# Graph aggregation by one-hot products: two PSUM banks for the moved products, tables and selectors on other engines, and a new order of the first lists

## The chip, the cores and the metric

One NeuronCore of a Trainium2 chip runs the kernel. The metric is device time in microseconds, the median of three runs. The profile is that of one execution, taken by the hardware profiler.

## The reference

Each of 65536 edges adds the feature row of its source node to the output row of its destination node. There are 4096 nodes with 128 float32 features each.

```python
num_nodes, num_edges, dim = 4096, 65536, 128
output = np.zeros((num_nodes, dim), dtype=np.float32)
for i in range(len(edge_index_src)):
    output[edge_index_dst[i]] += node_features[edge_index_src[i]]
```

## The kernel before

The kernel has no gather and no scatter. It sorts the edges with products of one-hot matrices, and then forms the output as a product of dense count blocks with the features. A node number is split into a block of 128 nodes (`>> 7`, 32 blocks) and a place in it (`& 127`).

**Preparation, first pass.** The edges lie on 128 partitions in six lists (`q` = 0 to 5, `NQ = 6`), each a column group of up to 22 × 4 edges per partition. The indices arrive by three transfers each for source and destination: list 0, list 1, and lists 2 to 5 together. For each list the kernel does the following, with the engine in brackets:

- `dst_keys(q)` [VectorE] shifts the destination to its block number. `buckets1(q)` [VectorE] compares it with a table of 32 block numbers and writes the one-hots `oh1`. The tables (`psi`, four slots of one PSUM bank) come from index vectors that GpSimd makes; `more_iotas` [VectorE] copies three of them there.
- `column_sums1(q)` [TensorE, L253] adds up the one-hots into `pst`, and `scan(q)` [VectorE, L265] runs a prefix sum over them.
- `count(q, n)` steps a generator: matmuls of the one-hots with a triangle [TensorE, L273 and L275; L307 and L311 for list 0] into `psc`, evicted by ScalarE (L278, L314) into `cum`. Lists 1 to 5 have eleven evictions, in six steps. The rest of the generator sums the four edges of a column group with the `lists` selector [TensorE, L292; L319 for list 0, 32 matmuls] and `take_ranks` [ScalarE, L299] copies the ranks out, twice.
- `codes()` [VectorE, L202, L204 and L206] packs the 7-bit places of source and destination and the source block number; `words(a, b)` [ScalarE, L212] turns these into the 32-bit words `kab` of lists a to b; `spread1(q)` [GpSimd, L333] multiplies the one-hots with them, in four instructions.
- `move1(q)` permutes the words to their rank: four groups `l`, each with three one-hots `p` of the rank [VectorE, L236] and about 22 products [TensorE, L356] into the PSUM tile `psm`, and at the end two copies [ScalarE, L360 and L361] out of `psm` into `sbk` and `sa`.

The order on each engine is written out by hand, and each engine works off its instructions in that order. While `move1(q)` goes on, `during(q)` puts work of later lists between its four groups: at `l = 0` the column sums of list q + 3, at `l = 1` the end of `count(q + 1)` (so its ranks) and `scan(q + 3)`, and two steps of `count(q + 2)` in each of the last three groups. `beside(q, l)` adds the start of the second pass, among it `sums0(2)` [TensorE, L461] in the last group of list 3 and `scan0(2)` [VectorE, L466] in the first of list 4.

PSUM has eight banks. Here they are shared by tag: "psA" (four buffers, count matmuls, fillers and later the blocks), "ps2", "pso", "misc" (one each) and "psi" (the tables). `psm` takes "misc" except for list 4, which takes a "psA". Column sums take "ps2" for even lists and "pso" for odd ones. `T0["x"]` of the second pass takes "ps2" early in list 2. `keep_busy(n)` issues n products of ones that nobody reads.

**Preparation, second pass,** and **the block of products.** The moved edges are sorted once more by destination group (`pass2`). Then 32 slots follow: one-hots of source and destination places [VectorE, `onehots`], their products, which are count blocks [TensorE, L769], a copy by ScalarE (L771), and the products of these with the features [TensorE, L776].

Of the kernel before, what the change touches and what calls it, by code (L numbers as in the profile page):

```python
# [8 lines left out]
P = 128  # L9
# [8 lines left out]
NB = 32  # L18
# [64 lines left out]
def _fast(ctx, tc, X, src32, dst32, out, ident, fmax, flag_i, T):  # L83
# [86 lines left out]
    V.tensor_copy(out=psi[:, 0], in_=iota[:].bitcast(I32))  # L170

    def selectors():
        with nc.allow_low_precision(reason="zeros and ones"):
            for t, by in ((lists, "p (k b) -> p k b"), (dests, "p (b k) -> p k b")):
                V.tensor_reduce(out=t[:], in_=identb[:].rearrange(by, k=4), op=OP.add, axis=AX.X)

    def more_iotas(which):
        for i, t in which:
            V.tensor_copy(out=psi[:, i, :t.shape[1] // 2], in_=t.bitcast(I32))

    piota, piotas = psi[:, 0].bitcast(U16), psi[:, 1].bitcast(U16)
    pswap = psi[:, 3].bitcast(U16)
# [15 lines left out]
            in_=by_quad(d_lo)[:, q, :, :, None].to_broadcast([P, NJ, 4, 2]),  # L198
            scalar=7, op=OP.logical_shift_right)

    def codes():
        V.tensor_scalar(out=code_i, in0=s_lo, scalar1=127, scalar2=7,  # L202
                        op0=OP.bitwise_and, op1=OP.logical_shift_left)
        V.scalar_tensor_tensor(out=code_i, in0=d_lo, scalar=127, in1=code_i,  # L204
                               op0=OP.bitwise_and, op1=OP.bitwise_or)
        V.tensor_single_scalar(out=sblk_i, in_=s_lo, scalar=7, op=OP.logical_shift_right)  # L206

    def words(a, b):
# [39 lines left out]
        onehot(oh1q(q), kd[:, q], NL, NB, io=pswap if q % 2 else piota)  # L248

    def column_sums1(q):  # L250
        pst = ps.tile([P, 512], F32, name="pst", tag=("ps2", "pso")[q % 2], bufs=1)
        for j in range(NJ):
            PE.matmul(out=pst[:, j:j + 1],  # L253
                      lhsT=oh1q(q)[:, 4 * j:4 * j + 4, :].rearrange("p l b -> p (l b)"),
                      rhs=ones[:, :1], start=True, stop=True)
        sums[q] = pst
# [23 lines left out]

    def counts_by_two(q):

        cum = sb1.tile([P, NJ, P], BF16, name="cum", tag=f"c{q % 2}")
        col = oh1q(q).rearrange("p (j l) b -> p j (l b)", l=4)
        for j0 in range(0, NJ, 4):
            js = range(j0, min(j0 + 4, NJ))
            before_by_two(col[:, j0:js.stop], cum[:, j0:js.stop],
                          [sums[q][:, j - 1:j] if j else minus[:] for j in js[::2]])
            yield
        psr = ps.tile([P, 512], F32, name="psr", tag="psA", bufs=4)  # L290
        for j in range(NJ):
            PE.matmul(out=psr[:, 4 * j:4 * j + 4], lhsT=cum[:, j], rhs=lists[:],  # L292
                      start=True, stop=True)
        take_ranks(q, psr)
# [5 lines left out]

    def counts(q):

        cum = sb1.tile([P, NB, NL], BF16, name="cum", tag=f"c{q % 2}")
        for j0 in range(0, NJ, 4):
            n = min(4, NJ - j0)
            psc = ps.tile([P, 512], F32, name="psc", tag="psA", bufs=4)
# [36 lines left out]
    sbk = sb1.tile([P, NCH, NB], BF16, name="sbk")  # L343

    def move1(q, meanwhile):
        tag, bufs = ("psA", 4) if q == NQ - 2 else ("misc", 1)
        psm = ps.tile([P, 512], F32, name="psm", tag=tag, bufs=bufs)
        for l in range(4):
            t = p1[l // 2]
            n = QN[q]  # L350
            for j0, j1, m0, m1 in WIN:
                j1 = min(j1, n)
                onehot(t[:, l % 2, j0:j1, m0:m1], rank1[q][:, l, j0:j1], j1 - j0, m1 - m0, m0=m0)
            meanwhile(l)
            for j in range(n):
                PE.matmul(out=psm[:, l * 64:(l + 1) * 64], lhsT=t[:, l % 2, j, :],  # L356
                          rhs=v1[q][:, 4 * j + l].bitcast(BF16),
                          start=j == 0, stop=j == n - 1)
        pv = psm[:, :256].rearrange("p (l b k) -> p l b k", l=4, k=2)
        S.copy(out=sbk[:, place(q), :], in_=pv[:, :, :, 0])  # L360
        S.copy(out=sa[:, place(q), :], in_=pv[:, :, :, 1])  # L361
# [21 lines left out]
    def leave(k, pso):  # L383
# [6 lines left out]
        for h, copy, queue, tag in parts:  # L390
            psx = ps.tile([P, 512], F32, name="psx", tag=tag, bufs=1)
            for i in range(2):
# [4 lines left out]
                out=out[(4 * k + 2 * h) * P:(4 * k + 2 * h + 2) * P, :].rearrange(  # L397
                    "(i p) f -> p i f", p=P), in_=rows[:, 2 * h:2 * h + 2])

    dst_keys(0)  # L400
    buckets1(0)
    load_x()
    column_sums1(0)
    keep_busy(6)
    more_iotas([(1, iotas[:]), (2, iota4[:].rearrange("p s k -> p (s k)"))])
    scan(0)
    selectors()
    more_iotas([(3, iotax[:].rearrange("p s k -> p (s k)"))])
    for q in range(1, NQ):
        dst_keys(q)  # L410
    codes()
    buckets1(1)
    count(0, 4)
    words(0, 1)
    spread1(0)
    count(0, 2)
    words(1, NQ)
    keep_busy(16)
    column_sums1(1)
    spread1(1)  # L420
    buckets1(2)
    count(0)
    scan(1)
    column_sums1(2)
    buckets1(3)
    count(1, 6)
    scan(2)
    column_sums1(3)

# [5 lines left out]
    def start0():  # L435
        T0["o"] = sb1.tile([P, NCH, NB, 4], BF16, name="oh0", tag="oh0")
        both = sb1.tile([P, 2, NCH, NB, 4], BF16, name="vc0", tag="o0")
        T0["v"], T0["c"] = both[:, 0], both[:, 1]
        T0["s"] = sb1.tile([P, NCH], F32, name="sums0")
        T0["r"] = rank2[:, 0]  # L440
        T0["p"] = ps.tile([P, 512], F32, name="pst0", tag="pso", bufs=1)
        T0["x"] = ps.tile([P, 512], F32, name="ps0", tag="ps2", bufs=1)

    def keys0(q):
        cs = place(q)
# [85 lines left out]
    def beside(q, l):  # L531
# [23 lines left out]
        if (q, l) == (5, 1):  # L555
            x_part(2, 0)
        if (q, l) == (5, 2):
            ranks0(EARLY0[0], T0["x"][:, 384:], 2)
            x_part(0, 1, (0,))
            payloads0(4)  # L560
# [438 lines left out]
```

## Time and profile before

| what | value |
|---|---|
| median of three runs | 272.2 us (270.98, 272.2, 272.39) |
| the profiled execution | 271.35 us |
| its span | 269.7 us |
| TensorE, matmuls | 259.0 us busy (96%) |
| VectorE | 243.7 us busy (90%) |
| ScalarE | 192.8 us busy (71%) |
| GpSimd | 194.2 us busy (72%) |

Busy time is summed over the span from the first instruction to the last; the profiled execution's own time is 1.65 us longer than its span. The names in the profile: PE is TensorE's matmuls and PEld its weight loads, DVE is VectorE, ACT is ScalarE, POOL is GpSimd and SP is SyncE. L253 is line 253 of the kernel.

### The profile page before, as it was taken

How to read it: one execution, taken by the hardware profiler on the slowest of the kernel's cores; microseconds unless marked ns; L12 is line 12 of the kernel's file. 1: busy time of each engine (PE TensorE's matmuls, PEld its weight loads, DVE VectorE, ACT ScalarE, POOL GpSimd, SP SyncE). 2: the span in 40 equal slices, each digit the busy share in tenths (PEclk: the TensorE clock that was granted, in tenths of full speed). 3: DMA queues.
4: the chain of work that ended last, by engine and by line, in shares of the span. 5: the costliest groups of instructions: out<-in, count | busy, mean ns of one | idle time of the engine just before them, and what ended most of it. 6: DMA issues, size and time to landing. Idle time of an engine off the chain costs nothing.

```text
span 269.7 us, 7795 instructions
## 1 busy us (share of the span) xinstructions
PE 259.0 (96%) x3322; PEld 219.1 (81%) x3323; DVE 243.7 (90%) x261; ACT 192.8 (71%) x437; POOL 194.2 (72%) x198
## 2 busy tenths in 40 slices
PE   8899899889999999999999999999999999999993
PEld 7788888767888888888788888887888888878882
DVE  7999989999999999999999998999898899889601
ACT  2787799567867568785777677767777785868761
POOL 3498889999899999999899989999799200000000
PEclk9999999999999999999999999999999999999999
DMA  5900000000000010010001000100010001001001
GB/s 161 296 14 7 2 2 2 4 2 4 0 4 2 0 41 0 2 39 2 2 0 41 1 2 2 41 2 0 2 39 2 0 8 33 5 0 41 0 4 39
DMA packets 10068, 5.75 MB, mean 21 GB/s; under 512 B 304, under 2 KB 10032, under 8 KB 10032
## 3 DMA queue, kind: packets, MB, share of 16 engines
q1 hardware_dynamic: 8944, 4.59, 6.1%
q10 hardware_dynamic: 1088, 0.66, 0.9%
q8 instruction: 26, 0.43, 0.6%
q14 instruction: 10, 0.08, 0.1%
HBM read 3.15 MB, written 2.10 MB: 19 GB/s over the span
## 4 chain that ended last, share of the span: by engine, by line
PE 78%; DVE 8%; ACT 2%; issue 1%; DVEq 0%
PE pso L776 45%; PE psa L769 21%; DVE p L236 4%; PE ps L694 4%; PE psr L678 2%; PE psb L643 2%; DVE p2a L236 1%; PE psx L375 1%; DVE oh L236 1%; PE psm L356 1%; DVE oh L617 1%; DVE oh L446 0%; ACT xr L221 0%; PE psc L722 0%; PE psc L273 0%
## 5 line engine op out<-in xcount | busy, mean ns | idle before, releaser
L771 ACT CAST a<-psa 128x512 fp32r<-128x512 f32 x256 | 131.8, 604 | 26.2 <-PE psa L769 25.9
L776 PE MATMUL pso<-a,xr 128*128 128x512 f32 x512 | 134.7, 404 | 0.1
L776 PEld LDWEIGHTS pso<-a,xr 128*128 128x128 f32 x512 | 91.0, 189 | 17.0 <-ACT a L771 0.8
L236 DVE TENSOR_TENSOR oh<-psi,slo 128x4096 bf16<-128x4096 uint16 (+2 forms) x38 | 73.9, 1945 | 7.9 <-PE psa L769 7.9
L236 DVE TENSOR_TENSOR oh<-psi,dlo 128x4096 bf16<-128x4096 uint16 (+2 forms) x38 | 73.8, 1942 | 0.0
L769 PE MATMUL psa<-oh 128*128 128x128 bf16 x1024 | 68.2, 219 | 1.1 <-DVE oh L236 1.1
L769 PEld LDWEIGHTS <-oh 128*128 128x128 bf16 x1024 | 57.8, 98 | 13.1 <-issue 10.5
L626 POOL TENSOR_TENSOR v<-oh,sa 128x512 bf16<-128x512 bf16 x42 | 42.6, 1054 | 0.0
L665 POOL TENSOR_TENSOR cum<-cum,oh 128x512 bf16<-128x512 bf16 x36 | 40.6, 1169 | 0.0
L333 POOL TENSOR_TENSOR v<-oh,kab 128x704 f32<-128x704 bf16 x24 | 32.9, 1404 | 10.3 <-ACT kab L212 6.9
L236 DVE TENSOR_TENSOR p<-psi,rank 128x448 bf16<-128x448 uint16 (+3 forms) x72 | 29.6, 476 | 0.2 <-ACT rank L299 0.2
L356 PE MATMUL psm<-v,p 128*128 128x64 bf16 x512 | 19.8, 193 | 2.2 <-DVE p L236 1.8
L656 POOL TENSOR_TENSOR cum<-cum,two 128x256 bf16<-128x256 bf16 x25 | 19.3, 773 | 2.6 <-ACT cum L645 1.1
L356 PEld LDWEIGHTS <-p 128*128 128x128 bf16 x512 | 17.2, 98 | 3.7 <-DVE p L236 3.0
L278 ACT ACTIVATE cum<-psc,sums 128x256 bf16<-128x256 f32 x50 | 18.7, 504 | 0.0
L633 POOL TENSOR_TENSOR two<-oh 128x512 bf16<-128x512 bf16 x15 | 17.1, 1171 | 2.0 <-DVE oh L617 2.0
L660 POOL TENSOR_TENSOR cum<-cum,oh 128x512 bf16<-128x512 bf16 x15 | 17.0, 1161 | 0.0
L236 DVE TENSOR_TENSOR p2a<-psi,rank 128x3072 bf16<-128x3072 uint16 (+2 forms) x14 | 14.3, 1062 | 0.5 <-ACT rank L682 0.5
L236 DVE TENSOR_TENSOR p2c<-psi,rank 128x3072 bf16<-128x3072 uint16 x8 | 13.6, 1745 | 0.0
L273 PE MATMUL psc<-early,oh 128*128 128x256 bf16 x67 | 13.2, 272 | 0.2 <-ACT cum L278 0.2
L617 DVE TENSOR_TENSOR oh<-psi,sbk 128x3072 bf16<-128x3072 uint16 (+3 forms) x9 | 12.4, 1390 | 0.0
L275 PE MATMUL psc<-early,oh 128*128 128x128 bf16 x67 | 12.1, 219 | 0.0
(114 smaller groups left out, 240.8 us busy)
## 6 DMA issues: line engine op xcount, KB each, us to landing
xf<-in_node_features_dram SPq DMA_DIRECT2D x4, 512.0 KB, 5.8
out_dram<-rows SPq DMA_DIRECT2D x7, 256.0 KB, 2.2
raw<-in_edge_index_src_dram ACTq DMA_DIRECT2D x1, 336.0 KB, 5.6
raw<-in_edge_index_dst_dram SPq DMA_DIRECT2D x1, 336.0 KB, 5.4
raw<-in_edge_index_src_dram ACTq DMA_DIRECT2D x2, 88.0 KB, 2.7
raw<-in_edge_index_dst_dram SPq DMA_DIRECT2D x2, 88.0 KB, 2.5
out_dram<-rows SPq DMA_DIRECT2D x1, 128.0 KB, 1.8
out_dram<-rows ACTq DMA_DIRECT2D x1, 128.0 KB, 1.8
```

The source lines that it names most:

```text
L236: V.tensor_tensor(out=dst.rearrange("p i (m k) -> p i m k", k=2), in0=io.rearrange("p i (m k) -> p i m k", k=2), in1=keys2[:, :, None, :]. ...
L278: S.activation(out=cum[:, 2 * i:2 * i + 2].rearrange("p j e -> p (j e)"), in_=psc[:, 2 * i * P:2 * (i + 1) * P], func=RELU, bias=bias)
L333: G.tensor_tensor(out=v1[q][:, l::4], in0=oh1q(q)[:, l::4], op=OP.mult, in1=kab[:, q, l::4, None].to_broadcast([P, NJ, NB]))
L356: PE.matmul(out=psm[:, l * 64:(l + 1) * 64], lhsT=t[:, l % 2, j, :], rhs=v1[q][:, 4 * j + l].bitcast(BF16), start=j == 0, stop=j == n - 1)
L626: G.tensor_tensor(out=T2["v"][:, c:c + 4], in0=T2["o"][:, c:c + 4], op=OP.mult, in1=sa[:, c:c + 4, None, d0:d0 + 4].to_broadcast([P, 4, NB ...
L633: G.tensor_tensor(out=T2["t"][:, i:i + 4], in0=oh[:, i:i + 4, 0], in1=oh[:, i:i + 4, 1], op=OP.add)
L656: G.tensor_tensor(out=cum[:, :, 2 * i], in0=cum[:, :, 2 * i - 2], in1=two[:, :, i - 1], op=OP.add)
L660: G.tensor_tensor(out=cum[:, i:i + 4, 1], in0=cum[:, i:i + 4, 0], in1=oh[:, i:i + 4, 0], op=OP.add)
L665: G.tensor_tensor(out=flat("c")[:, c:c + 4], in0=flat("c")[:, c:c + 4], in1=flat("o")[:, c:c + 4], op=OP.mult)
L769: PE.matmul(out=psa[:, i * P:(i + 1) * P], lhsT=oh[:, 0, 4 * k + i, :], rhs=oh[:, 1, 4 * k + i, :], start=True, stop=True)
L771: S.copy(out=a[:, k, :], in_=psa[:])
L776: PE.matmul(out=pso[:], lhsT=xr[s // 16][:, s % 16, v, :], rhs=a[:, k, :], start=s == 0 and v == 0, stop=s == NB - 1 and v == 1)
```

## The change

The diff has four parts.

1. `psm` of lists 1 and 3 takes the tag "ps2"; lists 0, 2 and 5 stay in "misc" and list 4 in "psA". To make room, the column sums of list 4 go to "pso", and `T0["x"]` is allocated in list 5 instead of list 2.
2. `more_iotas` copies on ScalarE instead of VectorE. `selectors` no longer reduces on VectorE: `lists` comes from two selects, and `dests` from five additions of halves, all on GpSimd.
3. `codes` takes a range of lists: lists 0 and 1 come before the first scan, lists 2 to 5 after the second one-hots. The shift to source blocks is a function of its own, `src_blocks`, after them. `words` comes in three parts (list 0, list 1, lists 2 to 5) instead of two.
4. The order of the first lists is new: keys and one-hots of list 1 stand ahead of the keys of lists 2 to 5; column sums and scan of list 1 come sooner; the first step of its count stands ahead of the end of list 0's; its `cum` takes the tag "oh0" instead of "c1", which the raw indices hold. The fillers ahead of the counts go from 6 to 3, and those after them from 16 to 6.

```diff
     def selectors():
-        with nc.allow_low_precision(reason="zeros and ones"):
-            for t, by in ((lists, "p (k b) -> p k b"), (dests, "p (b k) -> p k b")):
-                V.tensor_reduce(out=t[:], in_=identb[:].rearrange(by, k=4), op=OP.add, axis=AX.X)
+        G.affine_select(out=lists[:], in_=ones[:, :4], pattern=[[-32, 4]], base=1,
+                        channel_multiplier=1, compare_op=OP.is_gt, fill=0.0)
+        G.affine_select(out=lists[:], in_=lists[:], pattern=[[32, 4]], base=32,
+                        channel_multiplier=-1, compare_op=OP.is_gt, fill=0.0)
+        t, n = identb, P // 2
+        while n >= 4:
+            to = dests if n == 4 else sb1.tile([P, n], BF16, name=f"fold{n}")
+            G.tensor_tensor(out=to[:], in0=t[:, :n], in1=t[:, n:], op=OP.add)
+            t, n = to, n // 2
 
     def more_iotas(which):
         for i, t in which:
-            V.tensor_copy(out=psi[:, i, :t.shape[1] // 2], in_=t.bitcast(I32))
+            S.copy(out=psi[:, i, :t.shape[1] // 2], in_=t.bitcast(I32))
...
-    def codes():
-        V.tensor_scalar(out=code_i, in0=s_lo, scalar1=127, scalar2=7,
+    def codes(a, b):
+        ts = slice(a * NL, b * NL)
+        V.tensor_scalar(out=code_i[:, ts], in0=s_lo[:, ts], scalar1=127, scalar2=7,
                         op0=OP.bitwise_and, op1=OP.logical_shift_left)
-        V.scalar_tensor_tensor(out=code_i, in0=d_lo, scalar=127, in1=code_i,
+        V.scalar_tensor_tensor(out=code_i[:, ts], in0=d_lo[:, ts], scalar=127, in1=code_i[:, ts],
                                op0=OP.bitwise_and, op1=OP.bitwise_or)
+
+    def src_blocks():
         V.tensor_single_scalar(out=sblk_i, in_=s_lo, scalar=7, op=OP.logical_shift_right)
...
-        pst = ps.tile([P, 512], F32, name="pst", tag=("ps2", "pso")[q % 2], bufs=1)
+        pst = ps.tile([P, 512], F32, name="pst", tag="ps2" if q in (0, 2) else "pso", bufs=1)
...
-        cum = sb1.tile([P, NJ, P], BF16, name="cum", tag=f"c{q % 2}")
+        cum = sb1.tile([P, NJ, P], BF16, name="cum", tag="oh0" if q == 1 else f"c{q % 2}")
...
-        tag, bufs = ("psA", 4) if q == NQ - 2 else ("misc", 1)
+        tag, bufs = {1: ("ps2", 1), 3: ("ps2", 1), NQ - 2: ("psA", 4)}.get(q, ("misc", 1))
...
+    selectors()
     dst_keys(0)
     buckets1(0)
     load_x()
     column_sums1(0)
-    keep_busy(6)
-    more_iotas([(1, iotas[:]), (2, iota4[:].rearrange("p s k -> p (s k)"))])
+    keep_busy(3)
+    more_iotas([(3, iotax[:].rearrange("p s k -> p (s k)")), (1, iotas[:]),
+                (2, iota4[:].rearrange("p s k -> p (s k)"))])
+    codes(0, 2)
     scan(0)
-    selectors()
-    more_iotas([(3, iotax[:].rearrange("p s k -> p (s k)"))])
-    for q in range(1, NQ):
+    dst_keys(1)
+    buckets1(1)
+    for q in range(2, NQ):
         dst_keys(q)
-    codes()
-    buckets1(1)
+    codes(2, NQ)
+    src_blocks()
     count(0, 4)
     words(0, 1)
     spread1(0)
+    column_sums1(1)
+    scan(1)
     count(0, 2)
-    words(1, NQ)
-    keep_busy(16)
-    column_sums1(1)
+    words(1, 2)
     spread1(1)
     buckets1(2)
+    count(1, 1)
+    keep_busy(6)
     count(0)
-    scan(1)
     column_sums1(2)
     buckets1(3)
-    count(1, 6)
+    count(1, 5)
+    words(2, NQ)
     scan(2)
     column_sums1(3)
...
-        T0["x"] = ps.tile([P, 512], F32, name="ps0", tag="ps2", bufs=1)
...
         if (q, l) == (5, 2):
+            T0["x"] = ps.tile([P, 512], F32, name="ps0", tag="ps2", bufs=1)
             ranks0(EARLY0[0], T0["x"][:, 384:], 2)
```

## Rows read from the trace of the kernel before

**Rows 1.** The chain of waits in order of time: start us, us, what.

```profile
58.71 0.62 PE psa L769 x8
```

**Rows 2.** Busy time by stretch; columns as the first line says.

```profile
core 0: us, PE busy (x) PEld busy (x) DVE busy (x) ACT busy (x) POOL busy (x), PEclk, DMA share, GB/s
...
14.10:29.00 14.90, 13.57 (x346) 12.66 (x343) 14.90 (x34) 13.12 (x40) 13.12 (x11) 1.00 0.02 6
...
68.00:265.00 197.00, 196.78 (x2053) 164.67 (x2050) 177.78 (x110) 142.76 (x303) 137.46 (x138) 1.00 0.04 11
```

**Rows 3.** Timeline of VectorE, the head: start us, us, engine, line, operation [idle before].

```profile
3.66 1.62 DVE L236 TENSOR_TENSOR oh<-psi,kd 128x2816 bf16<-128x2816 uint16 x1
...
6.15 0.20 DVE L265 TENSOR_TENSOR_SCAN sums<-ones,pst 128x22 bf16<-128x22 bf16 x1 [0.20 <-PE pst L253]
6.27 0.26 DVE L175 TENSOR_REDUCE lists<-identb 128x4 bf16<-128x128 bf16 x1
...
6.71 0.25 DVE L196 TENSOR_SCALAR kd<-raw 128x176 uint16<-128x176 uint16 x1
7.25 0.73 DVE L196 TENSOR_SCALAR kd<-raw 128x176 uint16<-128x176 uint16 x4 [0.29 <-DMA raw<-in_edge_index_dst_dram]
7.90 0.43 DVE L202 TENSOR_SCALAR raw<-raw 128x528 uint16<-128x528 uint16 x1
8.36 0.71 DVE L204 SCALAR_TENSOR_TENSOR raw<-raw 128x528 uint16<-128x528 uint16 x1
8.98 0.43 DVE L206 TENSOR_SCALAR raw<-raw 128x528 uint16<-128x528 uint16 x1
9.33 3.15 DVE L236 TENSOR_TENSOR oh<-psi,kd 128x2816 bf16<-128x2816 uint16 x2
...
14.12 0.37 DVE L236 TENSOR_TENSOR p<-psi,rank 128x448 bf16<-128x448 uint16 x1
```

**Rows 4.** Timeline of ScalarE, the head.

```profile
7.42 2.42 ACT L314 ACTIVATE cum<-psc,minus 128x512 bf16<-128x512 f32 x4 [3.58 <-PE psc L311]
9.72 0.48 ACT L212 ACTIVATE kab<-raw 128x88 uint16<-128x88 uint16 x2
10.05 1.06 ACT L314 ACTIVATE cum<-psc,minus 128x512 bf16<-128x512 f32 x2
10.98 1.28 ACT L212 ACTIVATE kab<-raw 128x440 uint16<-128x440 uint16 x2
```

**Rows 5.** Timeline of ScalarE, lists 1, 2 and 5.

```profile
18.36 0.40 ACT L299 CAST rank<-psr 128x88 bf16<-128x88 f32 x2 [0.29 <-PE psr L292]
...
22.79 0.36 ACT L361 CAST sa<-psm 128x128 bf16<-128x128 f32 x1
24.62 0.40 ACT L299 CAST rank<-psr 128x88 bf16<-128x88 f32 x2 [1.47 <-PE psr L292]
...
25.41 3.75 ACT L278 ACTIVATE cum<-psc,sums 128x256 bf16<-128x256 f32 x10
...
43.52 0.51 ACT L299 CAST rank<-psr 128x88 bf16<-128x88 f32 x2
```

**Rows 6.** Timeline of TensorE, first products of lists 1 and 3, sums of list 2.

```profile
23.25 0.80 PE L356 MATMUL psm<-v,p 128*128 128x64 bf16 x22 [0.64 <-DVE p L236]
...
35.86 0.77 PE L356 MATMUL psm<-v,p 128*128 128x64 bf16 x21 [0.45 <-DVE p L236]
...
39.57 0.24 PE L461 MATMUL pst<-ones,oh 128*128 128x1 bf16 x4
```

**Rows 7.** Timeline of VectorE, lists 1 to 5.

```profile
20.63 2.54 DVE L236 TENSOR_TENSOR p<-psi,rank 128x448 bf16<-128x448 uint16 x6
...
39.85 0.17 DVE L466 TENSOR_TENSOR_SCAN sums<-ones,pst 128x8 f32<-128x8 bf16 x1 [0.85 <-PE pst L461]
...
44.05 1.26 DVE L236 TENSOR_TENSOR p<-psi,rank 128x448 bf16<-128x448 uint16 x3 [0.20 <-ACT rank L299]
```

**Rows 8.** Timeline of TensorE, fillers and rank matmuls of list 0.

```profile
9.32 1.05 PE L150 MATMUL psw<-ones 128*128 128x128 bf16 x16
...
11.57 1.41 PE L319 MATMUL psr<-cum,identb 128*128 128x88 bf16 x32
```

**Rows 9.** Timeline of GpSimd, its first multiplies.

```profile
10.29 10.93 POOL L333 TENSOR_TENSOR v<-oh,kab 128x704 f32<-128x704 bf16 x8 [6.89 <-ACT kab L212]
```

More of the change, by code (lines that the diff above doesn't have):

```diff
@@ L301, in counts @@
     def counts(q):
-        cum = sb1.tile([P, NB, NL], BF16, name="cum", tag=f"c{q % 2}")
+        cum = sb1.tile([P, NB, NL], BF16, name="cum", tag="oh0" if q == 1 else f"c{q % 2}")
         for j0 in range(0, NJ, 4):
```

## The prediction, before the result was known

> **What bounds the kernel now.** I read the chain of waits first. It goes over to TensorE at 58.71 us and stays there to the end [rows 1]; before that it runs almost wholly on VectorE. The table by stage agrees: between 68 and 265 us TensorE is busy for 196.78 of 197.00 us, and between 14.1 and 29.0 VectorE for 14.90 of 14.90 [rows 2]. So the kernel is a preparation of some 57 us and then a block of products of fixed length. The diff touches the preparation alone, and what it is worth is by how much sooner that ends; a busy share over the whole span says nothing here.
>
> In the preparation VectorE has three places that are not plain work. One is its head, up to the first permutation one-hot (`p`) at 14.12 [rows 3]. The second is an idle 0.85 us ahead of the scan of list 2's column sums at 39.85, the third 0.20 us for the ranks of list 5 at 44.05 [rows 7]. Each has to be followed to the engine that is late.
>
> The second leads to TensorE: those sums (L461) run at 39.57 [rows 6], in a stretch that began late. The first product of a list starts at 23.25 after 0.64 us idle and, two lists on, at 35.86 after 0.45 [rows 6]; the list between is like them. The trace puts both down to `p` on VectorE. I don't believe it: six `p` instructions start at 20.63 and take 2.54 [rows 7], so the three of that first product are there at about 21.9. What does end 0.10 us ahead of 23.25 is ScalarE's copy out of `psm`: 22.79 + 0.36 = 23.15 [rows 5]. All `psm` up to list 3 have one bank ("misc"). So there is a loop: copies out of `psm`, first product, rank matmuls, ranks on ScalarE (24.62) [rows 5], eleven count evictions, copies again. Two turns take 12.61 us (23.25 to 35.86), 6.3 each, of which TensorE's own work is 5.66 (6.3 − 0.64); this is what makes the sums at 39.57 late.
>
> **Part by part. VectorE's head.** Two reductions and one copy between 6.27 and 6.71 go [rows 3]: 0.44. The two copies ahead of 6.15 lie in the wait for the first list's column sums and free nothing; `codes(0, 2)` goes into that place: a third of L202 (0.46 from start to start) and of L204 (0.62), 0.36 with nothing added, 0.5 with 0.07 for each start. The one-hots of list 0 end at 3.66 + 1.62 = 5.28, which leaves 0.87 us to the scan, so it fits. Afterwards `dst_keys(1)` (0.16, a quarter of the four from 7.25 to 7.90) and the second one-hots (1.53, half of 9.33 to 12.39) come ahead of the four keys that waited for the transfer until 7.25; that wait of 0.38 (6.71 + 0.16 to 7.25) goes. VectorE then runs: scan ends 6.27, keys 6.43, one-hots 7.96, four keys 8.61, codes of four lists (two thirds of 1.08) 9.33 to 9.38, source blocks (0.35) 9.71, scan 9.82, two one-hots 12.87.
>
> The next scan needs the third list's column sums, which TensorE runs behind the 32 rank matmuls of list 0. Those wait for ScalarE: its `words(0, 1)` stand ahead of the last two count evictions, and now wait for the source blocks, there at 9.79. Before, words started at 9.72 and evictions at 10.05 [rows 4]; now the evictions start at about 10.0, end at 11.06, and the matmuls run from 11.1 for 1.41 [rows 8] to 12.5. Before, they were held to 11.57 by the column sums of list 1, which now run at 8.0 to 8.6. Column sums of list 2 end at 13.1, the scan at 13.2, and the ranks, 0.40 on ScalarE [rows 5] after 12.5, at 12.95. The first `p` starts at 13.2 where it was 14.12: **0.9 us**. If TensorE's place isn't what it waits for, 12.98 and 1.1; if each new or split instruction costs another 0.1, 0.5.
>
> **The tables on ScalarE.** It sat idle 3.58 us up to 7.42 [rows 4], so three copies hide there. Their price isn't in the trace: below, half of the two rank copies in 0.40, above, 0.36 for 128 columns [rows 5]. If they must wait for the one-hots of list 0, which read the same bank to 5.28, they end between 5.9 and 6.4; the first reader is at 6.43. I take nothing, above 0.2. The Trainium skill (PSUM — Partial Sum Buffer, section PSUM bank collisions raise a hardware error) tells one to guard a bank against two engines at once, whatever the columns. By that the later figure holds and the copies have no overlap with the one-hots; no row here shows it yet.
>
> **Selectors on GpSimd.** Seven small instructions from 3.40 on, where GpSimd idles for 6.89 us [rows 9]. Were each as dear as one of its 704-wide multiplies (10.93 over 8, 1.37), they would end at 13.0 and its first multiplies 2.7 later; the first product waits for three `p` anyway, to 14.5, and needs only the first of them, at 14.4; list 1's last would be there at 24.0, and its product comes just ahead of list 2's first (27.5, below). Nothing, then.
>
> **Count of list 1 sooner, words in three parts.** `count(1, 1)` and two short `words` fill ScalarE between 11.1 and 12.1, where it waited for the rank matmuls. The other five steps of the count then need nine evictions from 13.5 (0.37 each, ten in 3.75 [rows 5]), to 16.85; the four-list `words` (two thirds to four fifths of 1.28 [rows 4], 1.0) end at 17.85; ranks of list 1 start at 17.85 instead of 18.36 [rows 5]. VectorE asks for them at 20.63 − 0.9 = 19.7. GpSimd's third spread needs the late words at about 21. Both are covered.
>
> **The banks.** Lists 1 and 3 go to "ps2", 0 and 2 stay in "misc". First products no longer wait for the copies, so the loop loses the copies and the product, 0.5 + 0.65 us of each turn. TensorE's first product of list 1 can start at about 21.4, of list 2 when `p` is there (27.5), of list 3 at 33.3 (35.86 before). The sums for 39.85 follow 3.7 to 4.1 later, 37.0 to 37.4; VectorE, earlier by 0.9, arrives at 39.0 − 0.9 = 38.1. **0.85 us** go. ScalarE, whose turn is then ranks 0.4, evictions 4.0, copies 0.5 and, from list 3 on, four further evictions and an `xr` copy, gives the ranks of list 5 at 41.4 to 41.9 (43.52 to 44.03 [rows 5]); VectorE comes for them at 43.85 − 0.9 − 0.85 = 42.1: **0.20 us**, with only 0.2 to spare. Putting off `T0["x"]` and the other new tags lengthens no wait that I can find: their last readers are done microseconds ahead.
>
> From 44 to 57 VectorE sets the pace and the others hang on it or on spreads that begin with it, so the gain passes through to the first product at 58.71.
>
> **Sum.** 0.9 + 0.85 + 0.2 = 1.95 us. The profiled execution took 271.35, of which 269.7 are span: 269.4. It lies 0.85 below the median of the three runs (272.2), and the four times have a mean of 271.7; I take 271.75 − 1.95 = **269.8 us**.
>
> **The rivals.**
> *The loop stays* (the first products did wait for `p`, as the trace says, or for something else that the banks don't change). Then only ranks of list 1, 0.5 sooner, start the loop earlier; VectorE saves 0.9 and stands 0.35 more at the scan: 0.5 us in all, 271.2. For it speaks the trace's own label, against it the 0.10 us from the copy's end to the product, too close for chance.
> *ScalarE becomes the bound.* Its margin is 0.2 us at list 5. If it is 0.8 later than worked out (words, evictions that wait for count matmuls), 0.6 of the gain goes: 270.4.
> *TensorE runs at its lower clock.* The fillers fall from 6 + 16 to 3 + 6. Granted now is 1.00, which is 2.4 GHz [rows 2]; the 16 at 9.32 covered 1.05 us [rows 8], and after them it waits some 0.5 us for the second one-hots (10.37 to 10.9); with six it stands idle for about 0.9 us ahead of 11.1. At 1.2 GHz the rank matmuls' 1.41 becomes up to 2.8 and TensorE's 5.3 us from 11.57 to 16.9 up to 10.6: ranks of list 1 some 4 late at 22 where VectorE asks at 19.7, which turns the gain of 1.95 into 0.35 lost; with part of the next list as slow, about 2 us lost, 273.7. It makes the kernel measurably slower from 3.3 us of delay on VectorE on. That the 0.5 us left the clock alone speaks against it. The Trainium skill (TensorE: Matmul & The Clock Gate, section Part 1: The HAM clock gate) says that the clock is released by activity and taken back by idleness; it favours this rival, though idle time as short as this would by that section leave it alone, as the rows do.
>
> **Numbers.** Forecast 0.60, loop stays 0.17, ScalarE 0.12, clock 0.07, something unseen 0.04. What a measurement here can tell from no change is 0.5%, 1.36 us: below 270.84 is faster. The forecast gives that in nine cases of ten (it has 0.6 us to lose, the runs differ by 1.4), ScalarE's in six, the loop's in few; the clock's is slower. Faster 0.65, same 0.25, slower 0.10. The range goes from 268.7 (head 1.1, and the lower runs of the kernel before) to 272.2 (the loop's 271.2 with the spread of the runs).
>
> **What would show it.** First `p` at about 13.2; no idle ahead of the scan at about 38 and of the first products, and those start before the copies out of `psm` end; ranks of list 5 under 42; first product of the block at 56.8 instead of 58.7; the block itself the same length. I am wrong if VectorE's idle time turns up elsewhere between 13 and 57, ahead of ranks or column sums above all, or if TensorE's matmuls before 17 us are longer than now.

## The result, and the profile after

The changed kernel takes 269.39 us (median of six runs, 269.29 to 269.49) where the kernel before took 271.81 beside it (270.98 to 272.41); the ratio is 0.9915 with a 95% interval of 0.9893 to 0.9936. The forecast was 269.8 in a range of 268.7 to 272.2. The kernel before falls into two groups, near 271.1 and near 272.3, and three of its six runs here were in the upper one; against the lower group, in which the profile shown above lies, the gain is 1.7 us, and the profiled executions differ by 1.87 (271.35 and 269.48; spans 269.7 and 267.9).

The table by stage of the changed kernel, with stages moved to earlier times by what the forecast gave; the columns are those of [rows 2].

```profile
13.20:28.00 14.80, 14.39 (x374) 13.54 (x370) 14.67 (x35) 13.72 (x42) 14.80 (x12) 1.00 0.07 17
28.00:42.10 14.10, 13.98 (x369) 13.21 (x365) 14.10 (x41) 12.86 (x39) 13.60 (x11) 1.00 0.01 4
...
66.00:263.00 197.00, 196.92 (x2055) 164.82 (x2052) 177.24 (x110) 142.69 (x303) 136.68 (x137) 1.00 0.04 11
```

The block of products is as long as it was (196.92 us of TensorE in 197.00, 196.78 in [rows 2]). Ahead of it VectorE is now busy for all of 28.0 to 42.1. The chain of waits of the changed kernel passes to TensorE here:

```profile
56.82 0.62 PE psa L783 x8
```

The block's first count blocks come at 56.82 where they came at 58.71 [rows 1]: 1.89 us sooner. (In both kernels the chain leaves TensorE again for about 0.9 us of ScalarE, from 64.55 before and from 62.67 now, and at the very end; the prediction's "to the end" passes over that, and nothing hangs on it.) VectorE's timeline, the head first and then the two scans by which the gain can be followed:

```profile
6.20 0.20 DVE L274 TENSOR_TENSOR_SCAN sums<-ones,pst 128x22 bf16<-128x22 bf16 x1 [0.29 <-PE pst L262]
6.31 0.23 DVE L202 TENSOR_SCALAR kd<-raw 128x176 uint16<-128x176 uint16 x1
6.64 1.62 DVE L245 TENSOR_TENSOR oh<-psi,kd 128x2816 bf16<-128x2816 uint16 x1
8.18 0.72 DVE L202 TENSOR_SCALAR kd<-raw 128x176 uint16<-128x176 uint16 x4
8.82 0.34 DVE L209 TENSOR_SCALAR raw<-raw 128x352 uint16<-128x352 uint16 x1
...
9.64 0.43 DVE L215 TENSOR_SCALAR raw<-raw 128x528 uint16<-128x528 uint16 x1
...
10.09 3.13 DVE L245 TENSOR_TENSOR oh<-psi,kd 128x2816 bf16<-128x2816 uint16 x2
13.35 0.20 DVE L274 TENSOR_TENSOR_SCAN sums<-ones,pst 128x22 f32<-128x22 bf16 x1
13.46 2.52 DVE L245 TENSOR_TENSOR p<-psi,rank 128x448 bf16<-128x448 uint16 x6
...
38.27 0.15 DVE L479 TENSOR_TENSOR_SCAN sums<-ones,pst 128x8 f32<-128x8 bf16 x1
...
54.14 0.24 DVE L727 TENSOR_TENSOR_SCAN sums<-ones,pst 128x12 bf16<-128x12 bf16 x2
```

The first `p` is at 13.46 instead of 14.12 [rows 3]: 0.66. The scan of list 2's column sums has no idle time ahead of it and is at 38.27 instead of 39.85 [rows 7]: 1.58, of which 0.92 came in between. The last scan of the preparation is at 54.14, and in the kernel before it was at 56.02:

```profile
56.02 0.25 DVE L713 TENSOR_TENSOR_SCAN sums<-ones,pst 128x12 bf16<-128x12 bf16 x2
```

That is 1.88. So the three places of the prediction gave 0.66, 0.92 and 0.30.

ScalarE's timeline (tables, words, evictions, ranks of lists 0, 1, 2 and 5, and the copy out of `psm` of list 0):

```profile
5.45 0.17 ACT L185 COPY psi<-iotax 128x16 int32<-128x16 int32 x1 [1.61 <-DVE xf L120]
...
9.15 0.32 ACT L221 ACTIVATE kab<-raw 128x88 uint16<-128x88 uint16 x1
10.10 0.30 ACT L221 ACTIVATE kab<-raw 128x88 bf16<-128x88 uint16 x1 [0.64 <-DVE raw L215]
10.29 1.03 ACT L323 ACTIVATE cum<-psc,minus 128x512 bf16<-128x512 f32 x2
...
12.82 0.40 ACT L308 CAST rank<-psr 128x88 bf16<-128x88 f32 x2 [0.44 <-PE psr L328]
...
17.82 0.44 ACT L308 CAST rank<-psr 128x88 bf16<-128x88 f32 x2
...
22.12 0.46 ACT L370 CAST sa<-psm 128x128 bf16<-128x128 f32 x1
22.87 0.40 ACT L308 CAST rank<-psr 128x88 bf16<-128x88 f32 x2 [0.29 <-PE psr L301]
...
40.97 0.67 ACT L308 CAST rank<-psr 128x88 bf16<-128x88 f32 x2
```

And TensorE's, the rank matmuls of list 0, the first products of lists 1 and 3, and list 2's sums:

```profile
11.37 1.41 PE L328 MATMUL psr<-cum,identb 128*128 128x88 bf16 x32 [0.99 <-ACT cum L323]
...
21.50 0.80 PE L365 MATMUL psm<-v,p 128*128 128x64 bf16 x22
...
33.09 0.78 PE L365 MATMUL psm<-v,p 128*128 128x64 bf16 x21
...
36.80 0.24 PE L474 MATMUL pst<-ones,oh 128*128 128x1 bf16 x4
```

The first product of list 1 starts at 21.50, 1.08 us ahead of the end of ScalarE's copy out of list 0's `psm` (22.12 + 0.46 = 22.58); before, it followed that end by 0.10 [rows 5, 6]. None of the first products of lists 1 to 3 has idle time ahead of it now, and the sums come at 36.80 instead of 39.57.

### The profile page after: what moved, and what is told of

Its sections match the earlier page's. It is cut to its first block, busy times and chain, and to the rows that moved or that the text cites. A ratio compares the mean times of both kernels' runs of the same rounds, so it can differ in the third digit from the quotient of the medians.

```text
span 267.9 us, 7775 instructions
## 1 busy us (share of the span) xinstructions
PE 258.7 (97%) x3310; PEld 218.3 (82%) x3310; DVE 242.3 (90%) x258; ACT 193.2 (72%) x442; POOL 195.5 (73%) x205
## 4 chain that ended last, share of the span: by engine, by line
PE 80%; DVE 15%; issue 2%; ACT 1%; DVEq 0%; POOL 0%; POOLq 0%
PE pso L790 46%; PE psa L783 21%; DVE p L245 9%; PE ps L708 4%; PE psr L692 2%; DVE oh L245 2%; PE psb L657 2%; PE psw L150 2%; DVE p2a L245 1%; PE psx L384 1%; DVE oh L459 1%; DVE oh L631 1%; PE pst L262 1%; PE psr L328 1%; PE psc L282 0%
## 5 line engine op out<-in xcount | busy, mean ns | idle before, releaser
L783 PEld LDWEIGHTS <-oh 128*128 128x128 bf16 x1024 | 57.8, 98 | 13.1 <-issue 11.1
L365 PE MATMUL psm<-v,p 128*128 128x64 bf16 x512 | 20.4, 193 | 0.6
L282 PE MATMUL psc<-early,oh 128*128 128x256 bf16 x67 | 13.2, 272 | 0.0
```

The costliest lines, as they stand in the source:

```text
L783: PE.matmul(out=psa[:, i * P:(i + 1) * P], lhsT=oh[:, 0, 4 * k + i, :], rhs=oh[:, 1, 4 * k + i, :], start=True, stop=True)
```

## The experiments

The kernels of a group shared the runs of the kernel before; its lower group was at 271.0 to 271.1 each time, so medians are also set beside the changed kernel's 269.39.

**The banks alone.** On the kernel before:

```diff
-        tag, bufs = ("psA", 4) if q == NQ - 2 else ("misc", 1)
+        tag, bufs = {1: ("ps2", 1), 3: ("ps2", 1), NQ - 2: ("psA", 4)}.get(q, ("misc", 1))
...
-        pst = ps.tile([P, 512], F32, name="pst", tag=("ps2", "pso")[q % 2], bufs=1)
+        pst = ps.tile([P, 512], F32, name="pst", tag="ps2" if q in (0, 2) else "pso", bufs=1)
...
-        T0["x"] = ps.tile([P, 512], F32, name="ps0", tag="ps2", bufs=1)
...
         if (q, l) == (5, 2):
+            T0["x"] = ps.tile([P, 512], F32, name="ps0", tag="ps2", bufs=1)
```

> The kernel before with the banks alone: moved products of lists 1 and 3 in ps2, column sums of list 4 in pso, T0 x allocated late. Theory (the first product of a list waits for ScalarE's copies out of the one bank): the idle time ahead of the first products of lists 1 to 3 goes, the scan of list 2's column sums no longer waits 0.85 us nor the one-hots of list 5 their 0.20, VectorE's head stays as it was (first p at 14.1): 1.0 us less, 270.8 beside a kernel before at 271.8. Rival (the first products wait for p, as the trace labels them): nothing, 271.8. The runs should still differ among themselves by over 1 us, since the keys of lists 2 to 5 still wait for the index transfer in VectorE's head.

Measured: 269.79 us, ratio 0.9949 (0.993 to 0.9969); nine runs from 269.64 to 270.08, three from 270.92 to 271.25. VectorE's timeline, list 2's scan and the one-hots that hold those of list 5:

```profile
38.89 0.16 DVE L465 TENSOR_TENSOR_SCAN sums<-ones,pst 128x8 f32<-128x8 bf16 x1
...
41.64 2.42 DVE L236 TENSOR_TENSOR p<-psi,rank 128x448 bf16<-128x448 uint16 x6
...
54.77 0.24 DVE L713 TENSOR_TENSOR_SCAN sums<-ones,pst 128x12 bf16<-128x12 bf16 x2
```

Both waits are gone, with the head as it was (first `p` at 14.09). The scan is 0.96 sooner than before and the last scan of the preparation 1.25 (54.77 for 56.02). The rival, that the first products wait for `p`, falls. The banks are worth 1.25 to 1.36 us (the nine lower runs have a median of 269.74, beside 271.1 for the lower group of the kernel before), more than the 1.05 that their idle times add up to.

**The rest alone.** The changed kernel with the old tags of `psm`:

```diff
-        tag, bufs = {1: ("ps2", 1), 3: ("ps2", 1), NQ - 2: ("psA", 4)}.get(q, ("misc", 1))
+        tag, bufs = ("psA", 4) if q == NQ - 2 else ("misc", 1)
```

> The changed kernel with the moved products of lists 1 and 3 back in misc. Theory (the loop through the one bank, not VectorE, sets list 2's column sums): VectorE is 0.66 us ahead at the first p, but the loop starts only 0.5 us sooner, with the ranks of list 1; VectorE stands about 1 us ahead of the scan, and 0.5 us is left of the gain: 271.3. Rival (the two parts add up, each worth what it is by itself): 0.8 us, 271.0, with no wait at the scan longer than 0.85. Runs closer together than those of the kernel before, since VectorE's head no longer waits for the index transfer.

Measured: 270.72 (270.62 to 270.76), ratio 0.9969 (0.9955 to 0.9982). The copies out of `psm` in ScalarE's timeline:

```profile
22.08 0.46 ACT L370 CAST sa<-psm 128x128 bf16<-128x128 f32 x1
...
28.49 0.36 ACT L370 CAST sa<-psm 128x128 bf16<-128x128 f32 x1
...
34.79 0.36 ACT L370 CAST sa<-psm 128x128 bf16<-128x128 f32 x1
```

the first products behind them in TensorE's:

```profile
22.64 0.80 PE L365 MATMUL psm<-v,p 128*128 128x64 bf16 x22 [1.04 <-DVE sums L274]
...
28.95 0.77 PE L365 MATMUL psm<-v,p 128*128 128x64 bf16 x21 [0.70 <-DVE p L245]
...
35.25 0.77 PE L365 MATMUL psm<-v,p 128*128 128x64 bf16 x21 [0.47 <-DVE p L245]
```

and VectorE's two waits and last scan:

```profile
39.24 0.17 DVE L479 TENSOR_TENSOR_SCAN sums<-ones,pst 128x8 f32<-128x8 bf16 x1 [0.94 <-PE pst L474]
...
43.46 1.26 DVE L245 TENSOR_TENSOR p<-psi,rank 128x448 bf16<-128x448 uint16 x3 [0.22 <-ACT rank L308]
...
55.44 0.24 DVE L727 TENSOR_TENSOR_SCAN sums<-ones,pst 128x12 bf16<-128x12 bf16 x2
```

The copies end at 22.54, 28.85 and 35.15, and each first product follows by exactly 0.10, whatever engine the label names (a scan, then `p`). So the loop through the bank is there again, as the theory has it. But it swallows next to nothing of the head. VectorE was 0.70 us ahead of the kernel before at the first `p` (13.42), and after a wait of 0.94 instead of 0.85 it is still 0.61 ahead at list 2's scan and 0.58 at the last one. The loop itself had moved: its first product came 0.61 sooner (22.64 for 23.25), behind ranks of list 1 that came 0.59 sooner (17.77 for 18.36). The time lies between the two expectations: the profiled execution took 270.74, 0.61 less than the one before, where the theory had 0.5 and the rival 0.8. And the two parts do add up, as the rival has it: 1.27 us for the banks and 0.61 for the rest in the profiled executions, where the whole change is worth 1.87; against the lower group of the same runs (271.1) it is 1.36 and 0.38, where the whole is worth 1.7.

**Fillers.** The changed kernel with the old numbers, and with none:

```diff
-    keep_busy(3)
+    keep_busy(6)
...
     count(1, 1)
-    keep_busy(6)
+    keep_busy(16)
```

> The changed kernel with the old numbers of fillers (6 and 16). Theory (TensorE keeps its clock with few fillers, and both places have room for the old number): the same time within 0.1 us, 269.4, with fillers of the same length each and the rank matmuls of list 0 at the same place. Rival (fewer fillers let the clock drop, or free TensorE for something late): a difference of 0.3 us or more either way, with matmuls of other length before 17 us.

Measured: 269.34 (269.3 to 269.41), ratio 0.9921 (0.99 to 0.9942): the same time.

```diff
-    keep_busy(3)
...
     count(1, 1)
-    keep_busy(6)
```

> The changed kernel without its 3 and 6 fillers. TensorE then stands idle for some 1.4 us ahead of the rank matmuls of list 0 (0.99 before). Theory (the clock falls in some executions when TensorE's idle stretch in the head is long enough, and the changed kernel lies just under that): part of the runs 0.5 to 1.5 us above the others with a mean granted clock under 0.995, the others at 269.4. Rival (the fillers keep nothing up): one group at 269.4, clock 0.995 or more.

Measured: 269.4, ratio 0.9937 (0.9917 to 0.9956); nine of ten runs from 269.31 to 269.41, at mean granted clocks of 0.996 to 1.0, and one at 271.16, at 0.997, so that its extra time isn't the clock's; what it is stays open. TensorE's idle stretch ahead of the rank matmuls was 1.32 us. In the new order the fillers do nothing that these runs can show.

**Tables and selectors back on VectorE.**

```diff
-            S.copy(out=psi[:, i, :t.shape[1] // 2], in_=t.bitcast(I32))
+            V.tensor_copy(out=psi[:, i, :t.shape[1] // 2], in_=t.bitcast(I32))
...
-    selectors()
     dst_keys(0)
...
     scan(0)
+    selectors()
     dst_keys(1)
```

(with `selectors` as two reductions on VectorE, as before).

> The changed kernel with the three table copies and the two selector reductions back on VectorE, the copies ahead of the first codes, the reductions behind the first scan. Theory (VectorE sets the pace from its head on): the first scan comes 0.3 to 0.5 us later, the reductions add 0.37, so the first p is 0.6 to 0.9 later and the kernel as much slower, 270.1. Rival (it is TensorE or ScalarE that first p waits for, with VectorE's work hidden): 0.2 or less, 269.5.

Measured: 270.08 (270.05 to 270.17), ratio 0.9951 (0.9932 to 0.997): 0.69 more than the changed kernel. Its first `p` is at 14.08, 0.62 later. So this part is worth 0.6 to 0.7 us on top of the rest. It can't be set down as one share of the head's gain: without it the kernel is 0.3 us slower than the banks alone in their lower group (269.74), so that the new order, with the tables in this place, costs time. With the tables on VectorE three copies stand ahead of `codes(0, 2)`, and the first scan comes 0.31 later (6.51 for 6.20).

**One more one-hot on VectorE.** List 3's one-hots are written twice.

```diff
     column_sums1(2)
     buckets1(3)
+    onehot(oh1q(3), kd[:, 3], NL, NB, io=pswap)
```

> The changed kernel with the one-hots of list 3 written twice, one more instruction of 1.53 us on VectorE ahead of the first p. Theory (VectorE sets the pace from its head to the block, and the other engines have room): all of it but the 0.2 us in which VectorE waits for column sums there, so 1.3 to 1.5 us more, 270.8. Rival (ScalarE or TensorE is just as tight in lists 1 to 5 and takes up part of a delay of VectorE): 0.9 us or less, 270.3.

Measured: 270.8 (270.72 to 270.95), ratio 0.9973 (0.9957 to 0.9989): 1.41 more for an instruction of 1.53. So a delay of VectorE there costs nearly all of itself. Whether VectorE alone sets the pace is another question, which the next kernel and the last one ask.

**Source blocks of lists 0 and 1 early.**

```diff
-    def src_blocks():
-        V.tensor_single_scalar(out=sblk_i, in_=s_lo, scalar=7, op=OP.logical_shift_right)
+    def src_blocks(a, b):
+        ts = slice(a * NL, b * NL)
+        V.tensor_single_scalar(out=sblk_i[:, ts], in_=s_lo[:, ts], scalar=7,
+                               op=OP.logical_shift_right)
...
     dst_keys(1)
+    src_blocks(0, 2)
     buckets1(1)
...
-    src_blocks()
+    src_blocks(2, NQ)
```

> The changed kernel with the source blocks of lists 0 and 1 ahead of the second one-hots, so that words of list 0 no longer wait 0.64 us on ScalarE; the count evictions behind them and the rank matmuls of list 0 come about 0.7 us sooner. Theory (VectorE sets the pace and waits for TensorE 0.2 us ahead of the third scan alone): 0.05 to 0.15 us less, 269.3. Rival (that chain through ScalarE and TensorE sets the first p): 0.5 us less or more, 268.8.

Measured: 269.1 (269.0 to 269.11), ratio 0.9907 (0.988 to 0.9934): 0.29 less than the changed kernel. Rank matmuls of list 0 and the scan that follows list 2's column sums:

```profile
10.48 1.41 PE L330 MATMUL psr<-cum,identb 128*128 128x88 bf16 x32 [0.26 <-ACT cum L325]
```

```profile
12.90 0.19 DVE L276 TENSOR_TENSOR_SCAN sums<-ones,pst 128x22 f32<-128x22 bf16 x1
```

The matmuls come 0.89 sooner, the scan 0.45 (0.30 counted from the first scan, which was 0.15 earlier in this execution). So the changed kernel's VectorE does wait for that chain, by 0.3, twice what I expected, but far from the rival's 0.5 or more.

**Keys of lists 2 to 5 on ScalarE,** on top of that:

```diff
+    def dst_keys_s(q):
+        S.activation(
+            out=kd[:, q].rearrange("p (j l) k -> p j l k", l=4),
+            in_=by_quad(d_lo)[:, q, :, :, None].to_broadcast([P, NJ, 4, 2]),
+            func=COPY, scale=1.0 / 128, bias=-63.5 / 128)
...
-    for q in range(2, NQ):
-        dst_keys(q)
...
     count(0, 4)
+    dst_keys_s(2)
     words(0, 1)
...
     count(0, 2)
+    dst_keys_s(3)
     words(1, 2)
...
     count(0)
+    dst_keys_s(4)
+    dst_keys_s(5)
     column_sums1(2)
```

> As the kernel with early source blocks, and the keys of lists 2 to 5 made by ScalarE (a scaled and shifted copy that is rounded to the block number) in its idle places. It takes 0.64 us off VectorE. Theory (VectorE's instructions up to the block are the time): first p at about 13.0 where it was 13.46 and 0.4 us less than the changed kernel, 269.0. Rival (ScalarE or TensorE has become as tight): no change or slower, 269.4 or more, with VectorE idle ahead of scans or p.

Measured: 268.93 (268.75 to 268.96), ratio 0.99 (0.9873 to 0.9927): 0.46 less than the changed kernel and the fastest here. VectorE's timeline:

```profile
9.59 3.16 DVE L253 TENSOR_TENSOR oh<-psi,kd 128x2816 bf16<-128x2816 uint16 x2 [0.19 <-ACT kd L208]
12.85 0.20 DVE L282 TENSOR_TENSOR_SCAN sums<-ones,pst 128x22 f32<-128x22 bf16 x1
```

Of the 0.64 us taken off VectorE only 0.17 shows over the kernel with early source blocks alone: VectorE now waits for the keys, and then again for list 2's column sums behind the rank matmuls. The first `p` is at 12.97, as expected, but it was at 13.01 already with the early source blocks. TensorE waits 0.54 us for ScalarE's evictions ahead of the rank matmuls, where it waited 0.26 with the early source blocks alone, so that ScalarE's row, which the keys themselves made longer, holds back the head here.

**Banks, and the keys later.** On the kernel with the banks alone:

```diff
-    for q in range(1, NQ):
+    dst_keys(1)
+    buckets1(1)
+    for q in range(2, NQ):
         dst_keys(q)
     codes()
-    buckets1(1)
```

> The kernel before with the banks, and the keys of lists 2 to 5 behind the one-hots of list 1. Runs of the kernel before, and with the banks alone, lie in two groups 1.2 to 1.4 us apart (271.1 and 272.3; 269.75 and 271.15), those of the kernels with the new order in one. Theory (in some executions the transfer for lists 2 to 5 lands later, and VectorE waits for it ahead of the list 1 one-hots): one group within 0.3 us, 0.3 to 0.4 below the lower group of the banks alone, 269.4. Rival (the two groups come from something else, such as the order of words or the fillers): two groups again over 1 us apart.

Measured: 271.36, ratio 0.9983 (0.9962 to 1.0004), and both halves of my theory fell. There are two groups, five runs from 270.35 to 270.47 and seven from 271.29 to 271.71, and they differ in the mean granted clock: 0.997 to 1.0 in the lower, 0.989 to 0.993 in the upper. And the lower group is 0.7 slower than with the banks alone, because `codes` now comes later and ScalarE's words with it:

```profile
10.27 0.65 ACT L212 ACTIVATE kab<-raw 128x88 uint16<-128x88 uint16 x2 [1.00 <-DVE raw L204]
```

TensorE then waits 1.56 us for the evictions ahead of the rank matmuls (11.88). So moving the keys doesn't pay by itself. The new order also has `codes(0, 2)` ahead of the first scan, where the words no longer wait for it; that this is what makes the moved keys pay is likely from these rows, but no run tried it alone. And the two groups are not the index transfer.

**The fillers of the kernel before.** The next two ask after the groups.

```diff
-    keep_busy(16)
```

> The kernel before without the 16 fillers ahead of list 1's column sums; TensorE then stands idle from 9.3 to 11.0 us. Runs of the kernel before lie in two groups: 271.0 to 271.4 at a mean granted clock of 0.997 to 1.0, and 272.1 to 272.7 at 0.993 to 0.994, a third of them. Theory (the upper group is TensorE at its lower clock behind its idle stretch near 10 us): most or all runs in the upper group, 272.2 or more at 0.994 or less, and a profile of one shows a granted clock under 1 in the head and rank matmuls of list 0 nearly twice as long as 1.41 us. Rival (the groups come from the index transfer or from elsewhere): a third in the upper group as before.

```diff
-    keep_busy(16)
+    keep_busy(28)
```

> The kernel before with 28 fillers in the place of the 16; they cover TensorE's idle stretch up to 11.0 us but for some 0.1. Theory (the upper group is TensorE at its lower clock behind that stretch): one group, 271.0 to 271.4 at a clock of 0.997 or more. Rival (the groups come from elsewhere): a third of the runs near 272.3 as before.

Measured: without them 271.67, ratio 1.0018 (1.0001 to 1.0034), nine of twelve runs at a clock of 0.990 to 0.994 (271.42 to 272.43) and three at 1.0 (271.04 to 271.34). With 28: 271.07, ratio 0.9994 (0.998 to 1.0008), one of thirteen runs at 0.993 (272.3), the others at 0.997 or more (270.84 to 271.39). The kernel before itself had 5 of 27 runs at 0.993 or 0.994 beside these two, and 22 of all 83 runs whose clock is on record; those 22 took 272.1 to 272.7 us and the other 61 at most 271.42. So the upper group is TensorE's clock. Taking the fillers away makes the lower clock come more often (9 of 12 against 5 of 27). That 12 more make it rarer isn't shown (1 of 13 against 5 of 27), and the theory's single group did not come. Nor did its times without the fillers: five of the nine took 271.9 to 272.4, the other four 271.4 to 271.8, and in the profiled one the rank matmuls took 1.67 us, not twice 1.41. And the one run with 28 that fell into the upper group is the profiled one, and it shows the place to be another than I thought (last section).

**The count of list 1 not sooner.**

```diff
     buckets1(2)
-    count(1, 1)
     keep_busy(6)
     count(0)
...
-    count(1, 5)
+    count(1, 6)
```

> The changed kernel with the first step of list 1's count back behind the end of list 0's. Two questions. Time: ranks of list 1 come some 0.7 us later, at 18.5, and VectorE asks for them at 19.9, so by the theory that VectorE alone sets the pace nothing changes (269.4); by the rival (ScalarE's chain is just as tight) 0.3 us or more. Clock: a profile of the kernel before with 28 fillers shows the clock at its lower level from 17.9 to 21.2 us, behind a stretch in which TensorE waits for the count evictions of list 1. If these waits bring it about, part of the runs here should lie about 1 us above the rest, with a mean granted clock under 0.995, since the waits are longer again; if it is something else in the old head, one group.

Measured: 269.75 (269.73 to 269.84, five runs), ratio 0.9948 (0.9934 to 0.9961): 0.36 more than the changed kernel. The theory that VectorE alone sets the pace falls. It is not the ranks that are late, for they are at 18.50 and still in time, but this:

```profile
16.17 0.20 DVE L274 TENSOR_TENSOR_SCAN sums<-ones,pst 128x22 f32<-128x22 bf16 x1 [0.23 <-PE pst L262]
```

List 3's column sums stand behind the count on TensorE and are late for their scan. No run had a clock under 0.995, but neither had the nine runs of the kernel before beside them, so on the clock this says nothing.

## Why the prediction was right, step by step

*VectorE's head*, 0.9 forecast, 0.66 measured. The mechanism holds: tables, selectors and the transfer's wait are off VectorE, and the first `p` waits for list 2's column sums, as worked out. The step that was too small is the start-to-start time of `dst_keys(1)`: I took a quarter of four keys in a row, 0.16, but the one-hots that read the keys start 0.33 behind them (6.31 to 6.64). With 0.05 in the first scan, which was later in this execution, and small excesses in the codes, source blocks landed 0.28 later than worked out (9.64 + 0.43 = 10.07 for 9.79), and words, evictions, rank matmuls (11.37 for 11.1) and the first `p` (13.46 for 13.2) came later with them.

About 0.3 us of this head belongs to the execution that was profiled. There VectorE waited for the index transfer (0.29 idle at 7.25 [rows 3]). In the profiles of the kernel before with 28 fillers and without the 16, whose VectorE has the same instructions in the same order, that wait is missing. With 28:

```profile
6.75 0.88 DVE L196 TENSOR_SCALAR kd<-raw 128x176 uint16<-128x176 uint16 x5
...
13.77 2.52 DVE L236 TENSOR_TENSOR p<-psi,rank 128x448 bf16<-128x448 uint16 x6
```

The first `p` is at 13.77 (13.84 without the 16), and against that the changed kernel's 13.46 is only 0.31 sooner. The forecast counted the wait of 0.38 as if every execution had it. That most executions of the lower group lack it, and that the gain is therefore 1.7 us there and 1.87 between the profiles, fits these numbers but wasn't tested.

*Tables on ScalarE*: nothing, as taken. The first copy starts at 5.45, behind the one-hots of list 0 that read the bank (3.73 + 1.62 = 5.35), though ScalarE was free from 3.84; the copies end at 6.12, within the forecast's 5.9 to 6.4. The Trainium skill (PSUM — Partial Sum Buffer, section PSUM bank collisions raise a hardware error) wants two engines kept off one bank at the same time, whatever the columns. This trace agrees: the copies go to other columns of the bank, and none overlaps the one-hots. *Selectors on GpSimd*: nothing; they end at 5.24.

*Count of list 1 sooner*: I priced its ranks (17.85 forecast, 17.82 measured) and called the rest covered. That was a miss, in the other direction: it also moves list 3's column sums, and taking it back costs 0.36. The ranks count too: with the old banks they are what starts the loop sooner.

*The banks*: 1.05 forecast, 1.22 in the traces. First products were forecast at 21.4 and 33.3 and came at 21.50 and 33.09; the sums at 37.0 to 37.4 and came at 36.80; ranks of list 5 at 41.4 to 41.9, and their two copies end at 41.64. The size was off because I took the idle times of 0.85 and 0.20 as the price. An idle time begins where the row before it ends, and VectorE starts an instruction some 0.08 us before the end of the one ahead of it when nothing holds it up: six `p` that take 2.42 are followed after 2.34, and above the one-hots at 6.64 that take 1.62 are followed after 1.54. Each wait costs that too: 0.92 and 0.30.

*The sum*: 1.95 forecast, 1.88 at the last scan, 1.87 in the profiled executions. The head was 0.24 too large and the banks 0.17 too small; that they cancel is luck. *The base* was wrong: 271.75 is a mean over both groups of the kernel before, so that 0.4 us of TensorE's lower clock went into the forecast. From the profiled execution alone the prediction has 269.4, and that is what the changed kernel takes.

*The rivals*: the loop did not stay (with the banks alone its waits are gone). Its price of 0.5 us for a change without the banks was near the 0.61 that the profiled executions show, though not by its working: ranks of list 1 came 0.59 sooner and the scan's wait grew by 0.09, where it had 0.5 and 0.35. ScalarE did not become the bound; with the keys of four lists added to it, TensorE waits longer for it. The lower clock did cost time, but in the kernel before: that its idle 0.5 us "left the clock alone" was true of the one execution that was profiled, and 22 of 83 others ran with a lower mean clock and took about 1.2 us more. The prediction took idle time as short as this to leave the clock alone; in those executions the clock fell all the same. Why the new order is free of this was not foreseen and isn't settled (last section).

## What to carry to other kernels

A wait's label is the last event that the profile can tie to it, so look for a row that ends a fixed small time ahead of every instance: here the copy out of a bank, 0.10 us, three times of three. Before pricing a stall, follow the loop that it belongs to, and ask what starts the loop: here the head's part of the change was worth 0.6 us with the one bank and with two (profiled executions), because it moved the loop's start along with VectorE. Price a wait at its idle time plus the overlap that it breaks (0.92 for an idle 0.85), and an instruction that reads what the one before it wrote at more than its share of a row of independent ones (0.33 for 0.16). And take a wait for a transfer from more than one execution before counting on it.

## What the runs showed of the hardware that I had not expected

TensorE's clock falls for some 3.4 us in part of the executions of the old order. The kernel without the 16 fillers, its profiled execution by stage (columns as in [rows 2]); TensorE had been idle for 1.79 us up to 10.72:

```profile
12.00:13.00 1.00, 1.00 (x26) 1.00 (x24) 1.00 (x3) 0.01 (x1) 1.00 (x2) 0.64 1.20 301
13.00:14.00 1.00, 1.00 (x25) 0.88 (x23) 1.00 (x3) 0.39 (x2) 1.00 (x1) 0.50 0.84 209
```

The granted clock is 0.50, the level of 1.2 GHz, from about 12.3 to 15.7. The fall comes 1.6 us after TensorE has taken up work again. The kernel with 28 fillers, which had no such idle stretch, shows it later:

```profile
16.00:17.00 1.00, 1.00 (x41) 1.00 (x38) 1.00 (x4) 1.00 (x4) 1.00 (x2) 1.00 0.00 0
17.00:18.00 1.00, 0.68 (x12) 0.42 (x9) 1.00 (x4) 0.72 (x2) 1.00 (x1) 0.93 0.00 0
18.00:19.00 1.00, 1.00 (x8) 0.80 (x7) 1.00 (x3) 0.72 (x3) 1.00 (x2) 0.50 0.00 0
```

There the clock is at 0.50 from about 17.9 to 21.2. Ahead of it stand only short waits for list 1's count evictions, of 0.16 to 0.24 us (TensorE busy for 0.78 of 15 to 16 us and 0.68 of 17 to 18). A first-list product group takes 1.38 us instead of 0.80:

```profile
19.07 1.38 PE L356 MATMUL psm<-v,p 128*128 128x64 bf16 x22
```

VectorE then stands 1.10 us ahead of a scan at 23.92, and the last scan of the preparation is at 56.97 where the profile of the kernel before has 56.02, although its first `p` was 0.35 sooner: some 1.3 us, about what sets the upper group apart. So the clock fell here without a long idle stretch. That the short waits bring the fall about isn't shown, for the profile of the kernel before has the same waits and keeps its clock:

```profile
15.00:16.00 1.00, 0.76 (x17) 0.61 (x16) 1.00 (x3) 1.00 (x4) 1.00 (x2) 1.00 0.01 4
...
17.00:18.00 1.00, 0.80 (x23) 0.60 (x19) 1.00 (x4) 1.00 (x3) 1.00 (x2) 1.00 0.00 0
```

What decides between the two executions stays open.

None of 70 runs of kernels with the new order had a mean clock under 0.995 (the 0.995 to 0.998 of some is, in the profile of the changed kernel, a fall after its last product), those with 1.32 us of idle time and with no fillers among them. Which part of the new order keeps the clock up isn't settled: it isn't the banks (three of twelve runs with the banks alone fell, and seven of twelve with the banks and the keys later), and the one kernel that took back the sooner count had only five runs. It wasn't tried further.
